# Hybrid encoder block: the first stage reordered, two gates by channels of x ahead of the memory's products

## The chip, the cores and the metric

One core of one Trainium2 chip runs the whole kernel in one launch. The metric is the device time in microseconds of one execution. TensorE (PE) does the matrix products, VectorE (DVE), ScalarE (ACT) and GpSimd (POOL) the elementwise work, and SyncE (SP) issues most of the transfers. PEld is TensorE's weight load.

## The reference

All arithmetic is float32. T = 1024 frames of D = 1024 channels, a memory of 256 tokens. Cut to what the first stage serves:

```
h = rmsnorm(x) * g                                  # x: (1024, 1024)
z = h @ w_in        # HGRN2 q, f, i, g; FoX q, k, v, f; memory q; 3 x 1024 gate logits
y_a = hgrn2(...)    # gated linear recurrence, 4 heads
y_b = fox(...)      # forgetting attention, 8 heads
mem_kv = (rmsnorm(mem) * gm) @ mem_kv_w             # 256 x 1024: keys and values
y_c = cross_attention(q, rmsnorm(keys), values)     # 4 heads
gates = sigmoid(gate_logits)                        # one per branch and channel
x = x + (sum of gate * (y @ w_branch)) @ w_out
x = x + convglu(rmsnorm(x) * gf)                    # up, causal conv of width 3, gelu, down
```

## The kernel before

**Precision.** Each float32 operand is split into a rounded high part (a cast, mostly on ScalarE) and a low part (a subtraction on VectorE). A product is three matmuls of 512 columns: high x high, high x low, low x high (`mm3`, lines 155 to 157). So each operand costs a pass on ScalarE and one on VectorE before TensorE can use it, and the second matmul needs the low part of the moving side.

**First stage.** It makes the operands `uh`, `ul` of x times its norm gain from the eight channel chunks `xk[k]` (128 channels x 1024 frames); the keys and values of the memory (`kv_chunk`: eight chunks of weights `wkv`, the first four for the keys, the others for the values; two banks of PSUM take each); the logits of the first two gates in `ORDER`, eight steps over the channel chunks (`gate_step`: two gates, two halves of 512 frames, three matmuls, so twelve per step); and the inverse norm of the rows, `rt`, from the eight row tiles `x_row` (`x_norm`: a square with a sum on ScalarE each). `rt` is transposed on TensorE, written to DRAM and read back to all partitions as `rx` (`spread_dma`). A gate's logits leave PSUM only as a product with `rx` (line 420).

**Order.** `SEQ` (line 41) names the steps in the order in which they are written: `k0` to `k7` key and value chunks, `x0` to `x7` operands of x, `g0`, `g1` weights of the two gates, `s0` to `s7` gate steps, `mn` the memory's norm, `mk` and `mv` the keys and values on their way out, `mr` the memory's rows, `xn` the norm of x. The framework's scheduler then places every instruction on its engine by a simulated time, keeping the dependences; `issue_after` adds an ordering. An engine runs its instructions in the order so made. SP issues the loads: memT and the first four weight chunks first, then the rest along `SEQ`, the rows of x last. Weight chunks and rows share six buffers (`row_tile`); split weights `wh`, `wl` have three each, raw weights two.

**After it.** Two more gates (`gates_early(NCOVER)`, the cover: 48 matmuls each) run while `differences()` makes the operands T1 to T4 of a fast block scheme out of `xk`: ScalarE first multiplies the eight chunks by the norm gain (line 582), VectorE subtracts, and each difference is split. T2 and T3 come after the first gates have left PSUM (line 588). Then seven `dense_unit`s, each of seven quarter products of twelve matmuls, use them: B11, B21, T1, T2 and so on in the first.

Of the kernel before, what the change touches and what calls it, by code (L numbers as in the profile page):

```python
# [8 lines left out]
F32 = mybir.dt.float32  # L9
# [5 lines left out]
P = 128  # L15
# [13 lines left out]
NCOVER, NPAIR = 2, 10  # L29
NFOX = [0, 3, 0, 3, 0, 3, 1]  # L30
# [10 lines left out]
SEQ = ("k0 k1 k2 k3 x0 x1 g0 x2 mr g1 k4 s0 s1 x3 s2 k5 x4 mn mk s3 k6 x5 s4 k7 mv x6 s5 x7 xn s6 s7").split()  # L41
# [65 lines left out]
def tile_block(ctx: ExitStack, tc: tile.TileContext, xT, memT, x_rows, mem_rows, vec, fbias, mats, hmask, w_cm, w_hi, w_fqk, w_fv,  # L107
# [31 lines left out]
    def col(i):  # L139
        return cv[:, i:i + 1]  # L140
# [12 lines left out]
    def mm3(ps, lh, ll, rh, rl, first, last, more=False):  # L153

        PE.matmul(ps, lh, rh, start=first, stop=False, skip_group_check=more)  # L155
        PE.matmul(ps, lh, rl, start=False, stop=False, skip_group_check=more)  # L156
        PE.matmul(ps, ll, rh, start=False, stop=last, skip_group_check=more)  # L157
# [77 lines left out]
    mt = p0.tile([P, KC, NM], F32, tag="mt", name="mt")  # L235
    def row_tile(name):
        return p0.tile([P, 2 * HB], F32, tag="wkv", name=name, bufs=6)

    wkv = [row_tile(f"wkv{q}") for q in range(4)]
    mem_row = [row_tile(f"mr{i}") for i in range(2)]  # L240
    wkv += [row_tile(f"wkv{q}") for q in range(4, 8)]
    x_row = [row_tile(f"xr{i}") for i in range(6)]
    x_row += [row_tile(f"xr{i}") for i in (6, 7)]
# [8 lines left out]
    rgw = []  # L252
    for what in SEQ:
        if what[0] == "x" and what != "xn":
            k = int(what[1])
            SP.dma_start(xk[k], xT[:, k, :])
        elif what == "mr":
            for i in range(2):
                SP.dma_start(mem_row[i], mem_rows[i])
        elif what[0] == "g":  # L260
            br, j = order[int(what[1])]
            rgw.append(raw_weights(w_cm[16 + 8 * br + j], KC * P))
        elif what in ("k4", "k5", "k6", "k7"):
            q = int(what[1])
            SP.dma_start(wkv[q], w_mkv[q])
    SP.dma_start(ident, mats[:, 0:P])
    for i in range(8):
        last_row = SP.dma_start(x_row[i], x_rows[i])
    G.memset(mhalf, -0.5)
# [34 lines left out]
    for k in range(KC):  # L304
        S.activation(umh[:, k, :], mt[:, k, :], AF.Copy, scale=col(C_GM + k))
        V.scalar_tensor_tensor(out=uml[:, k, :], in0=mt[:, k, :], scalar=col(C_GM + k),
                               in1=umh[:, k, :].bitcast(F32), op0=ALU.mult, op1=ALU.subtract)
# [7 lines left out]
    def x_chunk(k):  # L315
        late["x_cast"] = S.activation(uh[k], xk[k], AF.Copy, scale=col(C_GX + k))
        V.scalar_tensor_tensor(out=ul[k], in0=xk[k], scalar=col(C_GX + k), in1=uh[k].bitcast(F32),
                               op0=ALU.mult, op1=ALU.subtract)
# [23 lines left out]
    def kv_chunk(i):  # L342

        what, q = i // 4, i % 4
        if q == 0:
            pkv[what] = [ps_proj(), ps_proj()] if what else [ps_tr(), ps_tr()]
        wh, wl = weights(None, (2, HB), wkv[i], parts=1 if i else 2)
        for kk in range(2):
            k = 2 * q + kk
            for m in range(2):  # L350
                ms = slice(m * P, (m + 1) * P)
                mm3(pkv[what][m], umh[:, k, ms], uml[:, k, ms], wh[:, kk, :], wl[:, kk, :], k == 0, k == KC - 1)
# [7 lines left out]
    def mem_keys():  # L360
# [8 lines left out]
        for m in range(2):  # L369
            V.tensor_mul(h4(mkt[:, m, :]), h4(mkt[:, m, :]), mkr[:, 4 * m:4 * m + 4].unsqueeze(2).to_broadcast([P, 4, P]))  # L370
        for hh in range(2):
            ptr = ps_tr()
# [8 lines left out]
    gw, gps = [], []  # L381

    def gate_weights(i):
        gw.append(weights(None, (KC, P), rgw[i], [p0.tile([P, KC * P], F32R, tag=t, name=t) for t in (f"gh{i}", f"gl{i}")]))
        gps.append([ps_proj(), ps_po()] if i else [ps_lg(), ps_lg()])

    def gate_step(k):
        for i in range(2):
# [8 lines left out]

    steps = dict(k=kv_chunk, x=x_chunk, g=gate_weights, s=gate_step)
    named = dict(mn=mem_norm, mk=mem_keys, mv=mem_values, xn=x_norm)
    for what in SEQ:  # L400
        if what == "mr":
            continue
        if what in named:
            named[what]()
        else:
            steps[what[0]](int(what[1]))
    p0.release()

    home = {}
# [3 lines left out]
    mqd = tc.dram_tile([4, P, T], F32, name="mqd")  # L413

# [9 lines left out]
    early = iter([i for i in range(2, len(order)) if i < 2 + NCOVER or i >= 2 + NCOVER + NPAIR])  # L424
# [8 lines left out]

# [135 lines left out]
    row = ps1.tile([P, HB], F32, tag="fe", name="row", bufs=3)  # L569
    spread_dma(rx, rt, row[:8, :P], "rx")  # L570
    for i in range(2):
        for n in range(2):
            SP.dma_start(gd[i, n], gate(n, gps[i][n]))
    first_gates = late["gate"]

    def differences():

        b = []
        for k in range(4):
            for t in (k, k + 4):  # L580
                with tc.issue_after(late["square" if t > 3 else "x_cast"].ins):
                    S.activation(xk[t], xk[t], AF.Copy, scale=col(C_GX + t))
            b.append([xk[k + 4 * c][:, n * HB:(n + 1) * HB] for c in range(2) for n in range(2)])
# [4 lines left out]
        with tc.issue_after(first_gates.ins):  # L588
# [4 lines left out]
        with tc.issue_after(first_gates.ins):  # L593
# [14 lines left out]
    cover, families = gates_early(NCOVER), differences()  # L608
    next(cover)
# [1010 lines left out]
def _layout(inp):  # L1620
# [49 lines left out]
    o["w_cm"] = chunks(cm)  # L1670

# [52 lines left out]
```

## Time and profile before

| what | value |
|---|---|
| three runs | 1705.72, 1705.95, 1706.81 us (median 1705.95) |
| profiled execution | 1707.23 us, span 1705.5 us |
| TensorE busy | 1689.9 us (99%), 8941 matmuls |
| VectorE, ScalarE, GpSimd busy | 1142.3, 808.9, 325.7 us |
| moved by DMA | 227.17 MB |

The span runs from the first to the last recorded instruction. A row of the timeline has start, duration, engine, line, operation, output and inputs, shape, count, and in brackets the idle time before it and what ended that. Matmul durations overlap, so the pace is the distance between starts. A row of `x8: a/b/c` has the shortest, median and longest duration in nanoseconds. SPq rows are the issue of a transfer.

### The profile page before, as it was taken

What the parts mean: (1) busy time and instruction counts of PE and PEld (TensorE: products, weight loads), DVE (VectorE), ACT (ScalarE), POOL (GpSimd) and SP (SyncE); (2) the same over time, 40 slices, a digit from 0 to 9 for tenths busy, and PEclk for the clock granted to TensorE, in tenths of its full rate; (3) what the DMA queues carried; (4) which work ended last, traced back from release to release, by engine and by line L of the source; (5) the groups of instructions that cost most, each with busy time, mean ns of one, the idle gap of its engine ahead of it and who ended that gap; (6) DMA issues with size and microseconds to landing.
All of it is one profiled execution on the core that took longest, in us unless ns stands there. A gap on an engine that the chain in (4) does not pass through costs nothing.

```text
span 1705.5 us, 24256 instructions
## 1 busy us (share of the span) xinstructions
PE 1689.9 (99%) x8941; PEld 1449.0 (85%) x8941; DVE 1142.3 (67%) x2044; ACT 808.9 (47%) x1436; POOL 325.7 (19%) x419
## 2 busy tenths in 40 slices
PE   8999999999999999999999999999999999999998
PEld 6888899989898998888888888788888888888887
DVE  7656545665666655786856845987787887775654
ACT  8634456655464553776531333644443444533432
POOL 0100022443433331553310000211111111100000
PEclk9999999999999999999999999999999999999999
DMA  9533232221212111100336552566445345494772
GB/s 361 182 132 112 76 133 85 77 92 45 95 53 87 52 57 56 67 28 17 102 128 210 166 185 99 161 174 173 144 146 142 118 141 155 167 357 150 244 273 87
DMA packets 83207, 227.17 MB, mean 133 GB/s; under 512 B 9728, under 2 KB 12424, under 8 KB 83088
## 3 DMA queue, kind: packets, MB, share of 16 engines
q1 hardware_dynamic: 65040, 161.12, 26.8%
q0 software_dynamic: 18048, 64.50, 13.1%
q8 instruction: 70, 1.15, 0.3%
q14 instruction: 49, 0.40, 0.1%
HBM read 180.72 MB, written 67.93 MB: 146 GB/s over the span
## 4 chain that ended last, share of the span: by engine, by line
PE 96%; DMA 2%; DVE 1%; ACT 1%; SPq 0%; issue 0%; POOL 0%; POOLq 0%; ACTq 0%
PE pp L155 21%; PE pp L157 21%; PE pp L156 21%; PE lg L157 4%; PE lg L155 4%; PE lg L156 4%; PE tr L156 2%; PE tr L157 2%; PE tr L155 2%; PE po L877 1%; PE lg L836 1%; PE lg L835 1%; PE po L876 1%; PE po L157 1%; PE po L155 1%; PE po L156 1%
## 5 line engine op out<-in xcount | busy, mean ns | idle before, releaser
L155 PE MATMUL pp<-uh,wh 128*128 128x512 f32 x412 | 163.2, 396 | 0.3 <-ACT wh L161 0.3
L156 PE MATMUL pp<-ul,wh 128*128 128x512 f32 x412 | 162.9, 395 | 0.0
L157 PE MATMUL pp<-uh,wl 128*128 128x512 f32 x412 | 162.4, 394 | 0.0
L156 PE MATMUL pp<-wl,uh 128*128 128x256 f32 (+1 forms) x512 | 146.2, 286 | 0.0
L157 PE MATMUL pp<-wh,ul 128*128 128x256 f32 (+1 forms) x512 | 145.9, 286 | 0.0
L155 PE MATMUL pp<-wh,uh 128*128 128x256 f32 (+1 forms) x512 | 145.5, 285 | 0.0
L161 ACT CAST wh<-s 128x512 fp32r<-128x512 f32 x113 | 68.4, 620 | 155.7 <-PE pp L156 77.6
L161 ACT CAST wh<-raw 128x1024 fp32r<-128x1024 f32 (+2 forms) x76 | 67.5, 890 | 101.3 <-PE pp L156 85.7
L161 ACT CAST wh<-rw 128x512 fp32r<-128x512 f32 x87 | 53.3, 620 | 97.6 <-PE pp L156 58.1
L155 PEld LDWEIGHTS pp<-wh,uh 128*128 128x128 f32 x512 | 97.3, 190 | 1.3
L156 PEld LDWEIGHTS pp<-wl,uh 128*128 128x128 f32 x512 | 97.4, 190 | 0.9
L157 PEld LDWEIGHTS pp<-wh,ul 128*128 128x128 f32 x512 | 97.4, 190 | 0.9
L1369 POOL DMA_DIRECT2D rw<-in_w_up x44 | 24.1, 555 | 384.9 <-ACT sqs L1304 163.0
L161 ACT CAST dwh<-wr 128x1024 fp32r<-128x1024 f32 (+1 forms) x41 | 40.2, 980 | 116.0 <-PE tr L156 39.2
L169 DVE TENSOR_TENSOR wl<-raw,wh 128x1024 fp32r<-128x1024 f32 (+2 forms) x75 | 78.0, 1041 | 22.0 <-ACT wh L161 21.7
L155 PEld LDWEIGHTS pp<-uh,wh 128*128 128x128 f32 x412 | 77.5, 188 | 15.3 <-ACT wh L161 0.7
L157 PEld LDWEIGHTS pp<-uh,wl 128*128 128x128 f32 x412 | 77.5, 188 | 15.1
L156 PEld LDWEIGHTS pp<-ul,wh 128*128 128x128 f32 x412 | 77.5, 188 | 14.5
L851 ACT ACTIVATE pt<-pt,st 128x128 f32<-128x128 f32 (+3 forms) x64 | 49.7, 777 | 39.8 <-DVE st L848 32.8
L169 DVE TENSOR_TENSOR dwl<-wr,dwh 128x1024 fp32r<-128x1024 f32 (+1 forms) x41 | 46.3, 1129 | 30.3 <-ACT dwh L161 30.2
L853 POOL TENSOR_SCALAR pt<-pt,st 128x128 f32<-128x128 f32 (+3 forms) x64 | 51.0, 797 | 78.0 <-DVE st L852 57.6
L161 ACT CAST ph<-tr 128x512 fp32r<-128x512 f32 (+1 forms) x80 | 41.8, 544 | 39.8 <-PE tr L865 14.5
(501 smaller groups left out, 5121.0 us busy)
## 6 DMA issues: line engine op xcount, KB each, us to landing
rw<-in_w_up POOLq DMA_DIRECT2D x44, 512.0 KB, 4.7
sd<-in_w_dn POOLq DMA_DIRECT2D x30, 512.0 KB, 6.0
br<-yd SPq DMA_DIRECT2D x30, 512.0 KB, 5.5
raw<-in_w_cm SPq DMA_DIRECT2D x26, 512.0 KB, 3.4
gd<-gt SPq DMA_DIRECT2D x48, 256.0 KB, 2.0
gt<-gd SPq DMA_DIRECT2D x48, 256.0 KB, 2.7
yd<-fc SPq DMA_DIRECT2D x44, 256.0 KB, 2.5
wr<-sd SPq DMA_DIRECT2D x20, 512.0 KB, 4.5
```

The source lines that it names most:

```text
L155: PE.matmul(ps, lh, rh, start=first, stop=False, skip_group_check=more)
L156: PE.matmul(ps, lh, rl, start=False, stop=False, skip_group_check=more)
L157: PE.matmul(ps, ll, rh, start=False, stop=last, skip_group_check=more)
L161: return S.copy(out, in_)
L169: return (sub or V).tensor_sub(l, src, h.bitcast(F32))
L835: PE.matmul(ps[:, :w], qa[i][:, tsl], kh[i][:, s0:s0 + w], start=True, stop=False)
L836: fox_sets[p][3] = PE.matmul(ps[:, :w], qa[i][:, tsl], kl[i][:, s0:s0 + w], start=False, stop=True)
L851: S.activation(pt[:, :ns], pt[:, :ns], AF.Exp, bias=st[:, 2:3], accum_out=st[:, 3:4])
L853: G.tensor_scalar(pt[:, :ns], pt[:, :ns], st[:, 3:4], 0.0, ALU.mult, ALU.add)
L876: PE.matmul(o, vhl[:, sb, :], ph[:, src], start=(sb == 0), stop=False)
L877: PE.matmul(o, vhl[:, sb, :], pl[:, src], start=False, stop=last)
L1369: late["raw"] = G.dma_start(raw[:, 2 * i:2 * i + 2, :], src[:, 2 * i:2 * i + 2, :])
```

## The change

- `SEQ` now starts with the gates: `w0 x0 s0 w1 x1 s1 ...`. The weights of both gates lie interleaved by channel in a new input `w_first` (host layout) and come in four pieces of 1, 1, 2 and 4 channel chunks (`WFIRST`); x's first two chunks come and are split in halves.
- Memory operands (`u0` to `u7`, formerly made at the start) are made between the last steps. The key chunks `k0` to `k3` follow the last step, then the keys leave PSUM (`me`), a third gate runs (`c0`, formerly the first of the cover), the first two gates leave PSUM (`ev`), the value chunks `k4` to `k7` follow (their products after the third gate's), and `mv`, `mk`.
- The transposition of `rt` stands in the third gate, after the third channel chunk of its second half.
- Loads on SP: constants, x and gate weights, memT ahead of x6, then the memory's rows, the weight chunks and x's rows in turn. Eight buffers instead of six.
- Nine products of constants (128 x 128, float32), with no reader, stand ahead of everything on TensorE (`NDULL`); GpSimd sets their two operands.
- The eight scalings of x are on GpSimd, with no ordering.

```diff
+NDULL = 9
-SEQ = ("k0 k1 k2 k3 x0 x1 g0 x2 mr g1 k4 s0 s1 x3 s2 k5 x4 mn mk s3 k6 x5 s4 k7 mv x6 s5 x7 xn s6 s7").split()
+SEQ = ("w0 x0 s0 w1 x1 s1 w2 x2 s2 x3 s3 w4 x4 s4 x5 s5 u0 u1 x6 s6 u2 u3 x7 s7 u4 u5 mn u6 u7 k0 k1 k2 k3 me xn c0 ev k4 k5 k6 k7 mv mk").split()
+WFIRST = {0: (0, 1), 1: (1, 2), 2: (2, 4), 4: (4, 8)}
...
+    G.memset(mhalf, -0.5)
+    dull = p0.tile([P, P], F32, tag="row", name="dull")
+    G.memset(dull, 0.0)
+    for _ in range(NDULL):
+        PE.matmul(ps_tr()[:, :P], mhalf[:, 0:1].to_broadcast([P, P]), dull, start=True, stop=True)
...
     SP.dma_start(cv, vec)
-    for q in range(4):
-        w = 2 if q else 1
-        for i in range(2 // w):
-            sl, ws = slice(2 * q + i, 2 * q + i + w), slice(i * HB, (i + w) * HB)
-            SP.dma_start(mt[:, sl, :], memT[:, sl, :])
-            SP.dma_start(wkv[q][:, ws], w_mkv[q][:, ws])
+    load_x(0, 2, load_first)
+    load_first(1)
+    load_x(1, 2)
+    load_first(2)
+    load_x(2)
+    load_first(4)
+    load_x(3)
+    load_x(4)
+    load_x(5)
+    SP.dma_start(mt, memT)
+    load_x(6)
+    load_x(7)
+    for i in range(2):
+        mem_row.append(row_tile(f"mr{i}"))
+        SP.dma_start(mem_row[i], mem_rows[i])
+    load_wkv(0)
+    load_wkv(1)
     SP.dma_start(ones, mats[:, P:P + 1])
...
     SP.dma_start(ident, mats[:, 0:P])
     for i in range(8):
-        last_row = SP.dma_start(x_row[i], x_rows[i])
+        load_row(i)
+        if i in (1, 2):
+            load_wkv(len(wkv))
+        if i == 2:
+            br, j = order[2]
+            cover_raw = raw_weights(w_cm[16 + 8 * br + j], KC * P)
+    for q in (4, 5, 6, 7):
+        load_wkv(q)
...
     def gate_step(k):
-        for i in range(2):
-            for n in range(2):
+        h, l = gw[k // 4]
+        for n in range(2):
+            for i in range(2):
                 sl = slice(n * HB, (n + 1) * HB)
-                mm3(gps[i][n], gw[i][0][:, k, :], gw[i][1][:, k, :], uh[k][:, sl], ul[k][:, sl], k == 0, k == KC - 1)
+                ws = slice((k % 4) * 256 + i * P, (k % 4) * 256 + (i + 1) * P)
+                mm3(gps[i][n], h[:, ws], l[:, ws], uh[k][:, sl], ul[k][:, sl], k == 0, k == KC - 1)
...
+    def first_cover():
+        wh, wl = weights(None, (KC, P), cover_raw)
+        pss = [ps_proj(), ps_proj()]
+        for n, ps in enumerate(pss):
+            sl = slice(n * HB, (n + 1) * HB)
+            for k in range(KC):
+                late["cover"] = mm3(ps, wh[:, k, :], wl[:, k, :], uh[k][:, sl], ul[k][:, sl], k == 0, k == KC - 1)
+                if (n, k) == (1, 2):
+                    with tc.issue_after(late["cover"].ins):
+                        spread_dma(rx, rt, p0.tile([P, P], F32, tag="row", name="row")[:8, :], "rx")
+        for n, ps in enumerate(pss):
+            SP.dma_start(gd[2, n], gate(n, ps))
...
     def differences():
...
             for t in (k, k + 4):
-                with tc.issue_after(late["square" if t > 3 else "x_cast"].ins):
-                    S.activation(xk[t], xk[t], AF.Copy, scale=col(C_GX + t))
+                G.tensor_scalar(xk[t], xk[t], col(C_GX + t), 0.0, ALU.mult, ALU.add)
...
-    cover, families = gates_early(NCOVER), differences()
-    next(cover)
+    families = differences()
+    with tc.issue_after(late["wkv"].ins):
+        next(cover)
```

More of the change, by code (lines that the diff above doesn't have):

```diff
@@ L345, in kv_chunk @@
         if q == 0:
-            pkv[what] = [ps_proj(), ps_proj()] if what else [ps_tr(), ps_tr()]
-        wh, wl = weights(None, (2, HB), wkv[i], parts=1 if i else 2)
+            pkv[what] = [ps_tr(), ps_tr()]
+        wh, wl = weights(None, (2, HB), wkv[i])
         for kk in range(2):
@@ L351, in kv_chunk @@
                 ms = slice(m * P, (m + 1) * P)
-                mm3(pkv[what][m], umh[:, k, ms], uml[:, k, ms], wh[:, kk, :], wl[:, kk, :], k == 0, k == KC - 1)
+                with tc.issue_after(late["cover"].ins) if what else nullcontext():
+                    mm3(pkv[what][m], umh[:, k, ms], uml[:, k, ms], wh[:, kk, :], wl[:, kk, :], k == 0, k == KC - 1)
     def mem_values():
@@ L422, in gate @@
         return gt
-    early = iter([i for i in range(2, len(order)) if i < 2 + NCOVER or i >= 2 + NCOVER + NPAIR])
+    early = iter([i for i in range(3, len(order)) if i < 2 + NCOVER or i >= 2 + NCOVER + NPAIR])
     def gates_early(count):
@@ L568, in tile_block @@
     home["pool"] = ps1
[L569 to L574, printed above, removed]
+    first_gate = late["gate"]
     def differences():
```

112 lines of the change are left out of this document (65 added, 47 removed).

## The prediction

> **What bounds the kernel now.** I read the page first (shares and chain), then TensorE's timeline over the first 90 us, then the windows of the same stretch.
>
> ```profile
> PE 1689.9 (99%) x8941; PEld 1449.0 (85%) x8941; DVE 1142.3 (67%) x2044; ACT 808.9 (47%) x1436; POOL 325.7 (19%) x419
> ...
> PE 96%; DMA 2%; DVE 1%; ACT 1%; SPq 0%; issue 0%; POOL 0%; POOLq 0%; ACTq 0%
> ```
>
> TensorE is the bound: nothing but its idle or slow time can be won. The change removes no product of the computation, so its worth is what TensorE loses in the first 90 us, before and after.
>
> ```profile
> 5.29 1.22 PE L155 MATMUL tr<-wh,umh 128*128 128x512 f32 x2 [5.29 <-ACT wh L161]
> ...
> 6.73 0.63 PE L157 MATMUL tr<-wh,uml 128*128 128x512 f32 x1
> 7.16 0.63 PE L156 MATMUL tr<-wl,umh 128*128 128x512 f32 x1
> ...
> 9.86 0.40 PE L157 MATMUL tr<-wh,uml 128*128 128x512 f32 x1
> 10.55 0.73 PE L155 MATMUL tr<-wh,umh 128*128 128x512 f32 x2 [0.29 <-ACT wh L161]
> 11.81 0.50 PE L156 MATMUL tr<-wl,umh 128*128 128x512 f32 x1 [0.53 <-DVE wl L169]
> 12.14 0.40 PE L157 MATMUL tr<-wh,uml 128*128 128x512 f32 x1
> ...
> 24.24 0.40 PE L156 MATMUL po<-ul,gh 128*128 128x512 f32 x1
> 25.16 0.50 PE L157 MATMUL po<-uh,gl 128*128 128x512 f32 x1 [0.52 <-DVE gl L169]
> ...
> 54.30 0.39 PE L155 MATMUL pp<-uh,wh 128*128 128x512 f32 x1
> ...
> 57.70 0.39 PE L155 MATMUL pp<-uh,wh 128*128 128x512 f32 x1
> ...
> 59.06 0.27 PE L323 MATMUL tr<-ident,rt 128*8 128x128 f32 x1
> ...
> 84.15 0.39 PE L157 MATMUL pp<-uh,wl 128*128 128x512 f32 x1
> 85.21 0.50 PE L155 MATMUL pp<-T2h,wh 128*128 128x512 f32 x1 [0.68 <-ACT fe L466]
> ...
> 88.31 0.39 PE L156 MATMUL lg<-ul,wh 128*128 128x512 f32 x1
> 88.97 0.50 PE L155 MATMUL pp<-uh,wh 128*128 128x512 f32 x1 [0.28 <-ACT wh L161]
> ```
>
> A row's first number is its start. From 54.30 to 57.70 stand 16 products, so one of 512 columns costs 3.40/15 = 0.227 us. The losses against that pace: 5.29 before the first product; the first chunk's twelve take 5.29 to 10.09 (9.86 and one pace), 4.80 instead of 2.72, so 2.08, at 0.43 us each at first (6.73 to 7.16); then 0.46 until 10.55; 0.81 more than two paces until 11.81; and 0.10 for the restart (11.81 to 12.14). That is 8.74. Later: 24.24 to 25.16 loses 0.69, 84.15 to 85.21 loses 0.83, 88.31 to 88.97 loses 0.43, each with a restart of 0.10: 2.25. Together **11.0 us**. What the change can win lies inside these.
>
> **Part 1: gates by channels of x first.** The first product needed a chunk of memT and half a chunk of its weights; now it needs half of x's first chunk and an eighth of the two gates' weights. Arrivals are judged by bytes moved.
>
> ```profile
> 0.00:4.00 4.00, 0.00 (x0) 0.00 (x0) 0.64 (x6) 1.83 (x3) 0.30 (x5) 1.00 0.44 139
> 4.00:6.00 2.00, 0.71 (x2) 0.50 (x2) 1.63 (x7) 1.39 (x6) 0.00 (x0) 1.00 0.94 243
> 6.00:8.00 2.00, 2.00 (x6) 1.61 (x5) 1.27 (x5) 0.61 (x1) 0.00 (x0) 1.00 0.71 253
> 8.00:10.00 2.00, 2.00 (x7) 1.48 (x5) 0.88 (x2) 1.46 (x3) 0.00 (x0) 1.00 0.99 345
> 10.00:12.00 2.00, 1.18 (x5) 0.49 (x4) 1.47 (x2) 1.40 (x3) 0.00 (x0) 1.00 1.03 403
> 12.00:16.00 4.00, 4.00 (x18) 3.26 (x18) 3.36 (x6) 3.61 (x5) 0.00 (x0) 1.00 1.03 417
> ```
>
> ```profile
> 4.62 0.62 ACT L161 CAST wh<-wkv 128x512 fp32r<-128x512 f32 x1 [0.26 <-DMA wkv<-in_w_mkv]
> ...
> 9.45 1.05 ACT L161 CAST wh<-wkv 128x1024 fp32r<-128x1024 f32 x1 [0.33 <-DMA wkv<-in_w_mkv]
> ...
> 12.10 1.05 ACT L161 CAST wh<-wkv 128x1024 fp32r<-128x1024 f32 x1 [0.35 <-DMA wkv<-in_w_mkv]
> ...
> 82.44 1.14 ACT L161 CAST T4h<-t4s 128x512 fp32r<-128x512 f32 x2
> ```
>
> ```profile
> L316 ACT ACTIVATE uh<-xk,cv x8: 1138/1151/1158, 15.3 to 33.0; 128x1024 fp32r<-128x1024 f32 x8
> L317 DVE SCALAR_TENSOR_TENSOR ul<-xk,cv,uh x8: 1277/1280/1285, 16.5 to 36.7; 128x1024 fp32r<-128x1024 f32 x8
> ```
>
> The last column (GB/s) times the width gives, cumulatively, 0.56 MB by 4 us, 1.04 by 6, 1.55 by 8, 2.24 by 10, 3.04 by 12, then 0.417 MB per us. A cast starts later than the count says: the chunk that ends 1.64 MB (counted at 8.25) was cast at 9.45, the one that ends 2.42 MB (10.45) at 12.10, so 1.2 to 1.65 us later.
>
> *Start.* The first gate weights end at 0.46 MB, as did the half chunk cast at 4.62. In the written order their cast (a quarter of 1024 columns, about 0.45) comes first, then that of half of x0 (0.62 for 512 columns): the first product at 5.7, and the second, which needs the low part from VectorE (about 0.65), at 6.35. So the start comes no sooner than 5.29.
>
> *First steps.* A step (one channel chunk, two gates, two halves) is twelve products, 2.72 us. Steps 0 and 1 end at 6.35 + 23 x 0.227 = 11.55; x1's second half (1.38 MB, 7.35 + 1.2, then 0.6 and 0.65) is there by 9.8, wanted at 10.2. Step 2 needs x2, which ends 2.16 MB: counted at 9.8, cast at 11.0 to 11.4 by the old rate. The windows from 4 to 8 us are slow (243 and 253 GB/s, one with only 0.71 of the engines' time); at the 403 of 10 to 12 it would be 4 + 1.6/0.403 + 1.2 = 9.2. Nothing shows why they are slow, so I take the middle, 10.3, with 9.2 and 11.4 as ends. Then cast 1.15 and low part 1.28 let the second product of step 2 go at 12.75, and step 2 ends at 12.75 + 11 x 0.227 = 15.25. Its 36 products are 8.17 us of work: lost 7.1, and 0.3 for three restarts, **7.4**. By the early end nothing waits for x2: 6.35 + 35 x 0.227 = 14.3, loss 6.4 with restarts; by the late end 16.35, loss 8.5. From step 3 on x comes every 0.524/0.417 = 1.26 us against 2.72, so no wait, and the loss of 24 to 25 us goes: its weights come in parts much earlier.
>
> **Part 2: constant products ahead of the data.**
>
> ```profile
> L334 PE MATMUL tr<-ident,rt x16: 271/275/275, 1081.8 to 1083.5; 128*128 128x128 f32 x16
> ```
>
> ```profile
> 0.73 0.11 POOL L269 MEMSET mhalf<- 128x16 f32 x1 [0.29 <-POOLq L1713]
> ```
>
> ```profile
> L921 POOL MEMSET A<- 128x512 f32 x2 | 1.0, 527 | 0.0
> ```
>
> The nearest operation is line 334's: eight products leave 16 records in 1.7 us, 0.11 each, so one of the new nine takes 0.23 at full pace and 0.43 to 0.45 at the slow one: 3.9 to 4.1 us for nine. They follow two memsets (0.11 from 0.73, and at most 0.53), so run from about 1.2 to 5.2, while TensorE waits anyway. Cost: nothing as long as they end before 5.7. They should spend the slow time (2.08 us lost at about 0.2 a product is some ten products, 4.3 us) on products nobody needs.
>
> The Trainium skill ("TensorE: Matmul & The Clock Gate", "What's actually happening") says the clock opens after one busy window of 3.4 us that runs freely. By it a pause between the constant products and the data can spoil the window, the slow pace could last to about 12.4, and the time would be 1704.3; the trace shows one opening only.
>
> **Part 3: x scaled on GpSimd.** ScalarE loses eight scalings of 1.14 (34 to 38 and 52 to 56 us), where it bounds nothing: worth nothing. GpSimd gets eight of the form of line 853.
>
> ```profile
> L853 POOL TENSOR_SCALAR pt<-pt,st 128x1024 f32<-128x1024 f32 x8 | 9.0, 1128 | 19.0 <-DVE st L852 12.8 <-PE tr L867 6.2
> ```
>
> ```profile
> 225.55 2.02 POOL L165 TENSOR_SCALAR mvh<-mkv 128x1024 fp32r<-128x1024 f32 x1 [0.15 <-DMA mkv<-kvd]
> ```
>
> ```profile
> 225.43 1.23 DVE L169 TENSOR_TENSOR mkl<-mkv,mkh 128x1024 fp32r<-128x1024 f32 x1 [9.24 <-POOL mkh L165]
> ```
>
> ```profile
> L306 DVE SCALAR_TENSOR_TENSOR uml<-mt,cv,umh x8: 477/479/485, 4.2 to 14.7; 128x256 fp32r<-128x256 f32 x8
> ```
>
> That is 9.0 us, to 16 at the 2.02 of a GpSimd pass beside VectorE, on an engine with 0.00 busy from 4 to 16 us; they go in the order 0, 4, 1, 5, 2, 6, 3, 7, so seven of them wait for x4 (about 17 us). T1 is wanted at 79. Hidden, and VectorE's pass beside it kept its 1.23: cost nothing.
>
> The Trainium skill ("SBUF — State Buffer", "Who interferes with whom") says that a VectorE pass with two SBUF inputs and a GpSimd pass that reads SBUF exclude each other, whichever starts first. The row agrees for GpSimd; a rival below has the other side.
>
> **Part 4: the rest of the order.** The two waits of 84 to 89 us come from differences that pile up once rx is there, with TensorE waiting for a copy queued behind ScalarE's casts of T4 (82.44).
>
> ```profile
> 64.55 1.29 DVE L420 TENSOR_TENSOR gt<-lg,rx 128x512 f32<-128x512 f32 x2 [4.07 <-DMA rx<-rx_d]
> ```
>
> ```profile
> 52.36 1.66 POOL L174 TENSOR_TENSOR rt<-rt,mhalf 128x8 f32<-128x8 f32 x1 [1.83 <-DVE rt L173]
> ```
>
> ```profile
> L395 ACT ACTIVATE xr<-xr x8: 1048/1052/1061, 40.1 to 50.9; 128x1024 f32<-128x1024 f32 x8
> ```
>
> Now: steps 3 to 7 end at 15.25 + 13.6 = 28.9, the keys' four chunks at 39.8, and the transposition of rt stands 33 products later, at 47.3. rx follows as before, 5.5 us later (59.06 to 64.55), at 52.8. T2 is wanted after that cover (50.7), the values (61.6), 0.8 of transpositions, the second cover (73.3) and three quarter products: 81.4. The work that took 64.55 to 85 fits with 8 us to spare, so both waits (1.46) go; if not, they stay. The weights moved behind x on SP's queue: the first key chunk ends 7.93 MB, counted at 23.7, split by 27.5, wanted at 28.9. The fourth ends 11.1 MB: 35, wanted 37.1; its buffer waits for the first memory row's square, done by about 26. Cost nothing, but with only 1.5 to 2 us of cover.
>
> **Sum.** 11.0 - 7.4 = 3.6 us. The profiled execution took 1707.23 (span 1705.5), so one like it would take 1703.6; the three times have a median of 1705.95, giving **1702.3**.
>
> **Rivals.**
> - *rt comes late.* The squares of x's rows (40.1 to 50.9 before) are written behind the keys' evacuation. If ScalarE runs them there, they start at 39.8 + 2.4, take 8.4 back to back or the 11.9 seen, and rt follows 2.0 later: 52.6 or 56.1. TensorE stands at its transposition from 47.3: 5.3 or 8.8 lost, 1707.6 or **1711.1**. Past 50.9 for rt the change loses. For it: the written order. Against it: before, they were written ahead of the last steps and ran elsewhere, so the order on the engines is the scheduler's, and ScalarE has room from 29 us on.
> - *Data late*: x2 at the late end, gain 2.5: **1703.4**. For it: the measured windows.
> - *The clock opens no sooner*: the real products run slow for 4.3 us from 5.7; steps 0 and 1 end at 13.2, step 2 at 15.9 instead of 15.25: **1703.0**. The change then does not do what it says.
> - *GpSimd holds VectorE up*: in steps 4 to 7 VectorE needs 1.28 + 0.48 and waits 1.13, 2.89 against 2.72, with one more for the first: 0.8 us, **1703.1**.
> - *The differences pile up again*: 1.46 stay, **1703.8**.
>
> **Chances.** What a measurement of this kernel can tell from no change is about 0.2%, 3.4 us. My forecast (1700.8 to 1702.5) 0.50; data late 0.16, clock 0.07, GpSimd 0.05, differences 0.05, all within 0.2%: 0.33; rt late 0.17, slower. The range goes down to 1700.8 (the early end, with x0 cast ahead of the weights, 0.5 sooner) and up to 1707.6, the lower price of rt late.
>
> **What would show it.** Right: real products from about 5.7, at 0.227 from the first or second step; one wait for x2 near 12; none at 24, 84 and 88; rt's transposition with no idle time before it. Wrong: a wait over 2 us anywhere from 28 to 60 us, named by rt or by key weights; products at 0.43 after 7 us; or x2's cast after 12.

## The result and the profile after

The change makes the kernel slower: 1712.55 us (median of 7 runs, 1711.43 to 1716.77) against 1706.81 (7 runs, 1705.72 to 1708.67), a ratio of 1.0034 [1.0023, 1.0046], so 5.7 us lost where 3.6 were to be won. The profiled execution after is the longest of its seven (1716.77 us, span 1715.0); the difference to the median is explained below.

The page after, busy time and chain:

```profile
PE 1698.5 (99%) x8959; PEld 1455.9 (85%) x8959; DVE 1145.6 (67%) x2047; ACT 801.3 (47%) x1431; POOL 342.7 (20%) x428
...
PE 94%; DVE 2%; DMA 2%; issue 1%; ACT 1%; POOL 0%; SPq 0%; DVEq 0%; POOLq 0%
```

VectorE has gained a share of the chain (1% to 2%) and TensorE lost 2%. TensorE's timeline after shows where (in brackets the idle time before a row and what ended it):

```profile
5.17 0.50 PE L157 MATMUL lg<-uh,wh 128*128 128x512 f32 x1 [0.66 <-ACT wh L163]
...
14.63 0.50 PE L158 MATMUL lg<-ul,wh 128*128 128x512 f32 x1 [1.35 <-DVE ul L354]
...
18.69 0.50 PE L158 MATMUL lg<-ul,wh 128*128 128x512 f32 x1 [1.00 <-DVE ul L354]
...
28.82 0.50 PE L158 MATMUL lg<-ul,wh 128*128 128x512 f32 x1 [1.67 <-DVE ul L354]
...
55.25 0.27 PE L360 MATMUL tr<-ident,rt 128*8 128x128 f32 x1
...
85.34 0.50 PE L159 MATMUL lg<-T1h,wl 128*128 128x512 f32 x1 [1.00 <-DVE wl L171]
...
90.75 0.50 PE L158 MATMUL pp<-T2l,wh 128*128 128x512 f32 x1 [0.76 <-DVE T2l L171]
...
93.40 0.79 PE L157 MATMUL pp<-T3h,wh 128*128 128x512 f32 x1 [1.92 <-ACT wh L163]
...
95.63 0.63 PE L159 MATMUL pp<-T3h,wl 128*128 128x512 f32 x1
96.06 0.63 PE L157 MATMUL pp<-T3h,wh 128*128 128x512 f32 x1
```

Three things are new. Three waits for a low part of x, `ul`, from VectorE (4.0 us). Three waits of 85 to 94 us (3.7 us, before 0.96). And products 0.43 us apart behind the last of them (95.63 to 96.06). Counted against 0.2267 us for each product of 512 columns, TensorE has lost 9.9 us by 44.6 us before (start, idle time, restarts, slow products; the prediction's list leaves out some tenths of restarts) and 11.7 after. The low part that ended the first wait stands in VectorE's timeline after:

```profile
12.69 0.69 DVE L645 TENSOR_TENSOR xk<-xk 128x512 f32<-128x512 f32 x1 [0.95 <-POOL xk L642]
13.30 1.28 DVE L354 SCALAR_TENSOR_TENSOR ul<-xk,cv,uh 128x1024 fp32r<-128x1024 f32 x1
...
16.75 0.69 DVE L645 TENSOR_TENSOR xk<-xk 128x512 f32<-128x512 f32 x1 [1.03 <-POOL xk L642]
17.35 2.48 DVE L354 SCALAR_TENSOR_TENSOR ul<-xk,cv,uh 128x1024 fp32r<-128x1024 f32 x2
20.85 0.69 DVE L645 TENSOR_TENSOR xk<-xk 128x512 f32<-128x512 f32 x1 [1.02 <-POOL xk L642]
21.46 2.07 DVE L354 SCALAR_TENSOR_TENSOR ul<-xk,cv,uh 128x1024 fp32r<-128x1024 f32 x1
23.45 4.12 DVE L340 SCALAR_TENSOR_TENSOR uml<-mt,cv,umh 128x256 fp32r<-128x256 f32 x8
27.49 2.47 DVE L354 SCALAR_TENSOR_TENSOR ul<-xk,cv,uh 128x1024 fp32r<-128x1024 f32 x2
```

Line 645 is T1's subtraction. It reads chunks that GpSimd has scaled, so it waits for GpSimd; and the schedule puts it ahead of the next `ul`, which then waits behind it although its own input has long been there. The eight low parts of the memory (`uml`) stand ahead of another. On ScalarE and GpSimd after:

```profile
10.88 1.15 ACT L353 ACTIVATE uh<-xk,cv 128x1024 fp32r<-128x1024 f32 x1 [0.61 <-DMA xk<-in_xT]
```

```profile
10.63 2.02 POOL L642 TENSOR_SCALAR xk<-xk,cv 128x1024 f32<-128x1024 f32 x1 [1.70 <-DVE ul L354]
14.67 2.04 POOL L642 TENSOR_SCALAR xk<-xk,cv 128x1024 f32<-128x1024 f32 x1 [2.02 <-DVE ul L354]
```

The high part of x2 was done by 12.03; its low part began at 13.30. Later, VectorE again, after and then before:

```profile
61.27 1.29 DVE L460 TENSOR_TENSOR gt<-pp,rx 128x512 f32<-128x512 f32 x2 [3.74 <-DMA rx<-rx_d]
...
71.28 0.69 DVE L171 TENSOR_TENSOR wl<-raw,wh 128x512 fp32r<-128x512 f32 x1 [1.06 <-ACT wh L163]
...
74.96 0.69 DVE L540 TENSOR_TENSOR s<-raw 128x512 f32<-128x512 f32 x1 [1.46 <-DMA kvd<-mvf]
75.57 1.29 DVE L171 TENSOR_TENSOR T1l<-xk,T1h 128x512 fp32r<-128x512 f32 x2
...
90.02 0.68 DVE L171 TENSOR_TENSOR T2l<-xk,T2h 128x512 fp32r<-128x512 f32 x1
...
92.01 0.69 DVE L540 TENSOR_TENSOR s<-raw 128x512 f32<-128x512 f32 x1
```

```profile
57.99 2.49 DVE L169 TENSOR_TENSOR T1l<-xk,T1h 128x512 fp32r<-128x512 f32 x4
64.55 1.29 DVE L420 TENSOR_TENSOR gt<-lg,rx 128x512 f32<-128x512 f32 x2 [4.07 <-DMA rx<-rx_d]
...
79.32 1.28 DVE L169 TENSOR_TENSOR T2l<-xk,T2h 128x512 fp32r<-128x512 f32 x2
```

Before, T1 was split in the gap ahead of `rx`, and T2's last low part ended 16.0 us after the first gate (80.6). After, the gates stand ahead of T1: `rx` comes 3.3 us sooner, T1's split starts 17.6 us later, T2's ends 10.1 us later (90.7). The product of T3 that waits until 93.40 does not wait for T3, whose low parts end at 82.87, but for its weights. They are cast by ScalarE from a sum (`s`) that stands behind T2 on VectorE, at 92.01:

```profile
92.73 0.62 ACT L163 CAST wh<-s 128x512 fp32r<-128x512 f32 x1 [0.63 <-DVE s L540]
```

### The profile page after: what moved, and what is told of

It reads as the page before. It is cut to its first block, busy times and chain, and to the rows that moved or that the text cites. A ratio compares the mean times of both kernels' runs of the same rounds, so it can differ in the third digit from the quotient of the medians.

```text
span 1715.0 us, 24291 instructions
## 1 busy us (share of the span) xinstructions
PE 1698.5 (99%) x8959; PEld 1455.9 (85%) x8959; DVE 1145.6 (67%) x2047; ACT 801.3 (47%) x1431; POOL 342.7 (20%) x428
## 4 chain that ended last, share of the span: by engine, by line
PE 94%; DVE 2%; DMA 2%; issue 1%; ACT 1%; POOL 0%; SPq 0%; DVEq 0%; POOLq 0%
PE pp L157 20%; PE pp L158 20%; PE pp L159 20%; PE lg L158 4%; PE lg L157 4%; PE lg L159 4%; PE tr L157 3%; PE tr L158 3%; PE tr L159 3%; PE po L938 1%; PE lg L897 1%; PE lg L896 1%; PE po L937 1%; PE tr L925 1%; PE lg L1127 1%
## 5 line engine op out<-in xcount | busy, mean ns | idle before, releaser
L914 POOL TENSOR_SCALAR pt<-pt,st 128x128 f32<-128x128 f32 (+3 forms) x64 | 51.6, 806 | 78.1 <-DVE st L913 64.0
L902 DVE CUSTOM_DVE_ANT_0 pt<-lg,nf 128x512 f32<-128x512 f32 (+2 forms) x80 | 41.5, 526 | 28.4 <-PE lg L897 14.1
```

What stands on the lines that cost most here:

```text
L902: V.tensor_tensor_reduce(out=pt[:, s0 + lo:s0 + hi], in0=ps[:, lo:hi], in1=bias, op0=ALU.add, op1=ALU.max, scale=1.0, scalar=-3e38, accum_ ...
L914: G.tensor_scalar(pt[:, :ns], pt[:, :ns], st[:, 3:4], 0.0, ALU.mult, ALU.add)
```

## The experiments

All are timed beside the kernel before; "loss" is TensorE's by 44.6 us as above.

**Who holds up the low parts of x?** x scaled on ScalarE again, and T1's subtractions ordered behind the last low part of x:

```diff
 e1_act_scale
-                G.tensor_scalar(xk[t], xk[t], col(C_GX + t), 0.0, ALU.mult, ALU.add)
+                with tc.issue_after(late["square" if t > 3 else "x_cast"].ins):
+                    S.activation(xk[t], xk[t], AF.Copy, scale=col(C_GX + t))
...
 e2_t1_late
-            V.tensor_sub(b11, b11, b12)
+            with tc.issue_after(late["x_low"].ins):
+                V.tensor_sub(b11, b11, b12)
```

> Part 3 undone: x is scaled on ScalarE again, behind the squares and casts; all the rest as after. Theory Q (VectorE's queue: the subtractions of T1 stand between the low parts of x and each waits for a GpSimd scaling): the subtractions leave that place, the waits of TensorE for the low parts at 14.6 and 18.7 us (1.35 and 1.00) go, the one at 28.8 (1.67, behind the low parts of the memory) stays; excess over pace between 0 and 40 us falls by about 2.4 us. Theory G (the two engines hold each other up whenever both run): the same here, since GpSimd no longer runs; this run shows only whether Part 3 is where the 2.4 us come from. ScalarE gets 8 passes of 1.14 us back; the waits at 85 to 95 us (3.7 us) stay or grow. Time about 1710, 2 to 3 us under after.

> x stays on GpSimd, but the four subtractions of T1 are ordered behind the last low part of x on VectorE. Theory Q: the waits at 14.6 and 18.7 us go just as in the kernel that scales on ScalarE, each low part starts as its high part is there; excess over pace between 0 and 40 us falls by about 2.4 us. Theory G: GpSimd's eight scalings still run beside the low parts (11 to 35 us), the low parts still take up to 2.07 instead of 1.28 us, and more than half of the 2.4 us stay. By both the wait at 28.8 us (1.67) stays, and the waits at 85 to 95 us stay.

e1: 1710.58, ratio 1.0019 [1.0011, 1.0028]. e2: 1709.28, 1.0011 [1.0002, 1.0020]. In e1 no wait for `ul` is left, but one of 1.83 for the key's weights at 30.77 takes its place, with a slow stretch behind it (loss 11.1). In e2 the waits for `ul` shrink from 4.0 to 1.3 (0.93 of it behind the memory's low parts) and the loss to 8.9, with GpSimd still scaling. So it is the order on VectorE that costs, more than the passes on GpSimd. The groups by line of e1, then of e2, up to 42 us (busy time, mean ns):

```profile
L354 DVE SCALAR_TENSOR_TENSOR ul<-xk,cv,uh 128x1024 fp32r<-128x1024 f32 x6 | 7.5, 1283 | 1.6 <-ACT uh L353 1.5
```

```profile
L354 DVE SCALAR_TENSOR_TENSOR ul<-xk,cv,uh 128x1024 fp32r<-128x1024 f32 x6 | 9.3, 1592 | 0.6 <-ACT uh L353 0.6
```

Beside GpSimd's scalings a low part takes 1592 ns in the mean, without them 1283. That is real and smaller: 0.3 us for each of six.

**Part 3 alone**, in the kernel before (the same edit the other way):

> The kernel before with x scaled on GpSimd and nothing else (Part 3 alone, no order given to it). Cost nothing (as predicted) would be 1707.0. Theory Q: here too the subtractions of T1 stand between the low parts of x on VectorE and wait for GpSimd; the last low parts come late, TensorE waits for them between 25 and 42 us, 1 to 3 us longer in all: 1708 to 1710. Theory G: the same, but then the low parts that run beside a GpSimd pass also take longer themselves, about 2.07 instead of 1.28 us.

1710.28, 1.0024 [1.0014, 1.0033]; loss 12.1 instead of 9.9. VectorE's timeline in it:

```profile
19.81 0.69 DVE L584 TENSOR_TENSOR xk<-xk 128x512 f32<-128x512 f32 x1 [1.03 <-POOL xk L581]
20.42 2.06 DVE L169 TENSOR_TENSOR gl<-raw,gh 128x1024 fp32r<-128x1024 f32 x1
```

The same subtraction jumps in, now ahead of the gate weights' low part; TensorE waits 1.55 us for that at 22.54. The low part itself is also stretched here, 2.06 us instead of 1.22. Of the 3.7 us, 2.2 are lost by 44.6 us; most of the rest lies in the waits of 88 to 94 us (2.25 instead of 0.96). So the edit costed at nothing costs 3.7 us by itself, on a kernel without any of the other parts.

**More put behind x.** e2, with the memory's operands written behind the steps of x, their low parts also ordered behind the last of x, and several tiles elsewhere in memory:

```diff
...
+        with tc.issue_after(late["x_low"].ins):
+            V.scalar_tensor_tensor(out=uml[:, k, :], ...
...
```

> Three edits: the subtractions of T1 behind the last low part of x; the eight low parts of the memory behind them too; and the buffers of the first stage laid out so that the sums of the first family no longer lie over the buffer from which the memory's values are written out. Theory Q plus C (the differences of T are late because their casts stand in ScalarE's and VectorE's queues behind work that waits for transfers and released buffers, not because rx is late): all three waits before 40 us go (about 4 us), T1's casts come before 68 us instead of 71 and 75, and the waits of 85 to 95 us fall from 3.7 to 1.5 or less; without idle time there, the clock does not fall at 92.8 us. Time about 1705. Rival (rx at 61 us sets the differences, and layout has no part in it): the early 4 us go, the 3.7 us stay, time about 1708.

1711.11, 1.0023 [1.0014, 1.0032], worse than e2. The waits for `ul` are down to 0.2, but what was pushed back now holds up the keys:

```profile
33.71 0.79 PE L158 MATMUL tr<-wl,umh 128*128 128x512 f32 x1 [3.57 <-DVE wl L171]
```

**The constant products**: none in the changed kernel (`NDULL = 0`); the nine put into the kernel before; and there eight more between the memory's first two chunks.

> The nine constant products are left out; all else as after. If the losses simply add, the first ten or so real products run at 0.43 instead of 0.227 us and the time grows by 2.1 us, to about 1714.6. If VectorE's queue sets the pace up to 20 us (theory Q), the slow products only eat up the waits at 14.6 and 18.7 us: TensorE reaches the product that waits at 28.8 us within 0.3 us of after, and the time stays at 1712 to 1713. In the clock's rows: open at about 9.3 us instead of 4.1.

> The kernel before with nine constant products at its start and nothing else (Part 2 alone). If the slow pace is a loss of its own, its 2.08 us go: about 1705.0. If the next weights set the pace (the second weight chunk's first product waits at 10.55 us for a cast that waited for its transfer), TensorE only arrives there earlier and waits longer: the waits at 10.5 and 11.8 us grow from 1.1 to about 3 us, and the time stays at 1707.

> The kernel before with nine constant products at its start, as in the run on Part 2 alone, and eight more between the memory's first and second chunk, where TensorE waited 1.9 us for the next weights and the clock then fell to half for 3.41 us (10.77 to 14.18). Theory D (the idle time is what makes the clock fall): the clock stays open there, the products from 10.8 us on keep 0.227 us, and the time is that of before or a little under, 1706 to 1707, some 2 us under the kernel with the nine alone. Rival (the fall has another reason, such as the early opening): the clock falls again near 10.8 us, 1708.6.

e4: 1712.52, 1.0030 [1.0018, 1.0041], as the changed kernel itself. e7: 1708.65, 1.0010 [1.0001, 1.0019]. e11: 1706.87, 1.0001 [0.9992, 1.0010]. The windows of e7, then of e11 (width; TensorE's busy time first; after the engines the granted clock, DMA's share, GB/s):

```profile
7.36:10.77 3.41, 1.47 (x6) 0.78 (x6) 1.12 (x4) 2.11 (x4) 0.00 (x0) 1.00 0.98 354
10.77:14.18 3.41, 3.30 (x7) 2.13 (x8) 3.41 (x6) 3.19 (x6) 0.00 (x0) 0.50 1.04 413
```

```profile
7.36:10.77 3.41, 3.17 (x17) 2.52 (x18) 1.57 (x3) 1.48 (x4) 0.00 (x0) 1.00 1.01 387
10.77:14.18 3.41, 2.65 (x14) 2.00 (x13) 2.72 (x4) 3.31 (x6) 0.00 (x0) 1.00 1.05 418
```

In e7 the first chunk runs at full pace, and TensorE then stands until its next weights at 10.66 (1.94 us instead of 0.29). What the fast clock saves is waited away. And the granted clock falls to half in the window behind that wait. In the profiled execution of e7 (1707.07) this slow stretch costs nothing: by 44.6 us the loss is that of before. So the 2.1 us of the median stay unexplained: the four slowest of the eleven executions show a lower mean clock (0.998, the profiled one 0.999), but no trace shows where. With the gap filled (e11) the clock does not fall, and the time is that of before.

**The clock at 93 us.** Eight constant products put between T2's and T3's products in the changed kernel:

> The kernel after with eight constant products (about 1.8 us) between T2's and T3's products of the first pair, where TensorE waits 1.92 us and the clock then falls to half at 92.8 us. Theory D (idle time of about 2 us makes the clock fall): T3's wait shrinks to nearly nothing, the clock stays open there, its products take 0.23 instead of 0.43 us, and the time falls by 1.7 to 3.4 us, to 1709 to 1711; whatever happens near 239 us is not touched. Rival (the fall has another reason, or the constant products themselves delay T3): the fall stays, 1712 to 1713.

1710.71, 1.0022 [1.0012, 1.0032]. The changed kernel's windows, then e13's:

```profile
89.41:92.82 3.41, 1.32 (x5) 0.45 (x3) 3.31 (x7) 2.00 (x5) 1.04 (x2) 1.00 0.91 314
92.82:99.65 6.83, 6.25 (x14) 4.48 (x15) 6.83 (x12) 3.43 (x6) 0.00 (x0) 0.50 0.81 279
```

```profile
92.80:99.60 6.80, 6.20 (x28) 4.55 (x27) 6.80 (x12) 3.33 (x6) 0.00 (x0) 1.00 0.83 272
```

The constant products fill the wait, and T3's first product comes no sooner (93.27 against 93.40); only the fall is gone, and 1.8 us with it: half of one window of 3.41. The profiled execution after had two double windows (this one and one at 239.60), a mean clock of 0.996; the other six show 0.998 to 0.999, which leaves room for at most two single windows. At 1.7 us a window that accounts for its 4 us above the median.

**Who makes T2 and T3's weights late?** First, five kernels that bring T1 ahead: the values' products straight behind the keys' and the gates written behind T1 (e5); e5 with T1's subtractions behind `rt`'s root and the memory's load behind x (e6); the changed order with the gates written behind T1 (e9); e9 with e6's repairs (e10); e6 with x's rows loaded between the memory's weights (e12). The core of e9's edit:

```diff
+    first_gates()
+    first_gate = late["gate"]
...
-            V.tensor_add(t, a, b)
+            with tc.issue_after(late["T1l"].ins):
+                V.tensor_add(t, a, b)
```

> Only the written order of the later part of the stage is changed: the memory's values straight behind the keys (their weights loaded ahead of the rows of x), and the first gates, which wait for rx, written behind the casts of T1 as in before. Nothing is done about the first 40 us. Theory C (T1's casts are late because they are written behind gates that wait for rx and lie in memory that the values hold): T1's casts run ahead of the first gate, before 63 us instead of 71 to 76; the waits of 80 to 95 us fall from 3.7 to 1.5 or less, as in before; the clock does not fall near 92 us. The early waits (1.35, 1.00, 1.67) stay. Time about 1708. Rival (the differences are late only because rx is): rt's transposition stands about 5 us later here, rx comes at about 63 us instead of 61, so the waits of 80 to 95 us are 3.7 us or more and the time is 1712 or more.

> All three repairs: the values first and the gates behind T1 (as in the run on theory C); the subtractions of T1 behind the root for rx on VectorE, so that none stands among the low parts of x; the memory's load, casts and low parts behind those of x. Theory Q plus C: no wait over 0.6 us between 12 and 60 us, at most 1.5 us at 80 to 95 us, no fall of the clock; the excess over pace below 100 us is about 7 us against 11 in before, and the time 1703 to 1705, 2 to 4 us under before. Rival (GpSimd and VectorE hold each other up): the low parts of x still wait, 2 us or more stay before 30 us, time about 1706.

> The kernel after, with only the written order and the memory around T1 changed: the first gates and the cover's gates, which wait for rx, written behind T1's casts; the first operands and sums ordered behind T1's low parts; T1 laid over buffers that the rows of x release by 48 us. rt's transposition keeps its place among the cover's products. Theory C (the differences are late because T1's casts and low parts are queued behind work that waits for rx and for transfers): rx comes near 61 us as in after, T1's low parts by 68 us instead of 72 to 76, T2's low parts end less than 25 us behind rx instead of 29, the waits of 80 to 95 us fall from 3.7 to 1.5 or less, the clock does not fall near 92 us; the early waits stay: 1707 to 1709. Rival (rx alone sets the differences): T2's low parts still end 29 us behind rx, the 3.7 us and the fall of the clock stay, 1712.

> As the run before this one, and with the repairs of the first 40 us: T1's subtractions behind the root for rx, the memory's load, casts and low parts behind those of x. Theory Q plus C: excess over pace in the first 40 us about 5.3 us (8.7 in after), rx near 58 us, waits of 80 to 95 us at most 1.5 us, no fall of the clock before 1000 us: 1704 to 1705, about 2 us under before. Rival: as above, 1708 to 1709.

> As the run with all three repairs (values behind the keys, gates written behind T1, T1's subtractions late, the memory behind x), but with what went wrong there mended: the rows of x are loaded between the memory's weights, so that rt's transposition can stand right behind the values at about 52 us instead of 64; the keys' transpositions use a free bank instead of waiting 2.6 us for the values to be copied out; T1 lies over buffers that are free by 48 us. Theory C in its sharper form (what counts is the time from rx to the last low part of T3, 19 us in before with T1 done ahead of rx and 29 us in after): rx near 58 us, T1's low parts by 64 us, the last low parts of T2 and T3 by 80 us, no wait over 0.6 us between 60 and 100 us, no fall of the clock before 1000 us; loss in the first 40 us about 8 us as in that run: 1703 to 1705, 2 to 4 us under before. Rival (VectorE's queue finds another wait to stand at): idle time of VectorE of over 4 us between 58 and 75 us, waits of 3 us or more at 80 to 100 us, 1709 or more.

All miss, and all are slower than the change. e5: 1722.60, 1.0094 [1.0080, 1.0108]. e6: 1721.03, 1.0082 [1.0068, 1.0096]. e9: 1719.57, 1.0078 [1.0064, 1.0092]. e10: 1715.53, 1.0051 [1.0039, 1.0064]. e12: 1717.11, 1.0056 [1.0043, 1.0070]. The loss by 44.6 us is cured in e6 and e10 (8.3, 8.4); in e12 it is 7.8 ahead of a wait of 2.06 us for the values' weights that ends at 45.37. But in e9 and e10 T1's split, now at the head of VectorE's queue, waits for its own inputs with the gates behind it. In e5 and e6 it waits too (3.4 and 3.2 us), and `rt`'s transposition stands 9 to 12 us later than after (66.89 and 64.33), so these two don't test the order of VectorE alone. In e12 VectorE stands instead for weights (4.44 us) and, ahead of a sum, for a transfer (3.53). e10's VectorE:

```profile
66.33 1.30 DVE L514 TENSOR_TENSOR T1l<-xk,T1h 128x512 fp32r<-128x512 f32 x2 [5.92 <-ACT T1h L163]
71.04 0.69 DVE L459 TENSOR_TENSOR gt<-pp,rx 128x512 f32<-128x512 f32 x1 [3.41 <-PE pp L159]
```

T3's first product then waits 3.8 to 4.3 us in the five, with the clock at half behind it. Then VectorE's amount of work: four passes fewer after (T1 without its low parts; the products read its high parts in their place, so e14 leaves out T1's small term), and four more before.

```diff
 e14_less_vector
-            family_block("T1", k, b11)
+            cast(S, fam["T1"][0][:, k, :], b11)
...
 e15_before_more
+                V.tensor_sub(t4[k], b22, b12)
```

> The kernel after without T1's four low parts in the first stage (four VectorE passes of 0.6 us, 2.4 us in all); the products read T1's high parts in their place, so what is left out is the small term of T1. Theory C in its last form (VectorE's queue from rx to T3's weights is one chain, and each pass in it moves its end): the waits of 80 to 95 us fall from 3.7 to about 1.3 us, the clock does not fall near 92 us, 1707.5 to 1709.5. Rival (transfers or ScalarE set that end): the waits stay within 0.5 us of 3.7 and the time at 1712.

> The kernel before with four more VectorE passes of 128x512 (0.6 us each, their results are overwritten) among T2's differences, behind rx. Theory C in its last form: everything behind them on VectorE moves by 2.4 us, the two waits of 84 to 89 us grow from 0.96 to about 3.4 us, and with idle time of that size the clock may fall for 3.41 us (1.7 us more): 1709 to 1711. Rival (the waits of before are set by ScalarE's casts of T4 alone, VectorE has room): 1706.5 to 1707.5.

e14: 1709.37, 1.0014 [1.0005, 1.0023]. e15: 1709.57, 1.0016 [1.0007, 1.0025]. Four passes are 2.4 us (one starts 0.60 us behind another); put into the kernel before, they cost 2.8. Without them, T3's first product comes 2.2 us sooner than after (91.19 against 93.40). So VectorE sets the end of this stretch nearly one to one (15.00 of the 15 us from 80 to 95 busy in it before, 14.89 after). TensorE's wait for T3's weights in e14, then in e15:

```profile
91.19 0.50 PE L157 MATMUL pp<-T3h,wh 128*128 128x512 f32 x1 [1.28 <-ACT wh L163]
```

```profile
89.91 0.50 PE L155 MATMUL pp<-T3h,wh 128*128 128x512 f32 x1 [1.66 <-ACT wh L161]
```

Neither is followed by a fall of the clock in these two traces. That would explain why taking 2.4 us away after wins 3.2, but it is not shown: e14's profiled execution is the fastest of its eleven (1707.84, mean clock 1.000), and seven of the others show 0.999.

**The chain shortened.** T1's subtractions behind `rt`'s root, the memory's load and operands behind x, T3's subtractions ahead of `rx`, T1's casts and low parts ahead of the operands and sums of the first unit, T1 written ahead of the cover over buffers that come free early; the first two gates stay where they were:

```diff
+            with tc.issue_after(late["rstd"].ins):
+                V.tensor_sub(b11, b11, b12)
...
+        for k, (b11, b12, b21, b22) in enumerate(b):
+            with tc.issue_after(late["rstd"].ins):
+                V.tensor_sub(b12, b22, b12)
...
-        s1 = dense.sum_of(1, a21, a22)
+        with tc.issue_after(late["T1l"].ins):
+            s1 = dense.sum_of(1, a21, a22)
```

> The kernel after with the first 40 us repaired (T1's subtractions behind the root for rx, the memory's load, casts and low parts behind those of x), and with the chain from rx to the third difference's weights shortened, not only moved: T3's four subtractions, which don't need rx, done ahead of it; T1's casts and low parts ordered ahead of the operand and the sum that wait for the second half of the pair's weights and ahead of the cover's own gates; T1 and the sums laid over buffers that are free by 48 us. The first gates keep their place. Theory C: VectorE stands idle under 2 us between 58 and 90 us, T1's low parts end by 71 us, T2's by 84, the waits of 80 to 95 us are at most 0.8 us, the clock does not fall before 1000 us; the first 48 gate and key steps lose about 8 us as in the runs with that repair: 1703 to 1705, 2 to 4 us under before. Rival (one more wait at the head of VectorE's queue): waits of 2 us or more at 80 to 95 us, 1707 or more.

1704.90 (11 runs), 0.9989 [0.9980, 0.9998]: 2.0 us faster than before and 7.7 than the change, though by the bound of 0.2% hardly to be told from before. TensorE's waits up to 110 us in it (total, times, longest):

```profile
PE lg L157 <- ACT wh L163: 1.5, 2, 1.1
PE pp L159 <- DVE wl L171: 1.0, 1, 1.0
...
PE lg L158 <- DVE ul L353: 0.4, 2, 0.2
PE pp L157 <- ACT wh L163: 0.3, 1, 0.3
```

The loss is 8.0 and the clock stays up. The time came as expected, the way there did not: VectorE still idles 4.2 us between `rx` and T2 (3.4 of them for T1's cast), and about 2.4 us of waits remain at 84 to 89 us. They use up what the first 44.6 us won. The same product of T2 (the first of the second unit) starts in before, then in e16 at:

```profile
102.26 0.39 PE L155 MATMUL pp<-T2h,wh 128*128 128x512 f32 x1
```

```profile
102.30 0.39 PE L157 MATMUL pp<-T2h,wh 128*128 128x512 f32 x1
```

So by 102 us e16 has won nothing over before. Its 2.4 us in the two profiled executions come later: 0.3 by 230 us, 1.2 near 1080 us (the wait far behind, below) and 0.8 behind TensorE's last product, which starts 4.9 us before the end of the span in before and 4.0 in e16. That it beats before is luck, then: what the expectation named wins nothing over before. That it beats the change, which has the last two gains as well, comes from the repair.

## Why the prediction was wrong

**Where the 5.7 us come from.** By 44.6 us 1.8 (11.7 against 9.9). The waits of 85 to 94 us with their restarts 3.0 (4.5 against 1.5). The clock 1.8 (e13). That is 6.6. Back comes 1.2, which nothing in the prediction foresaw, from waits far behind (1.0 of idle time, the rest restarts); the windows after, then before:

```profile
1075.00:1105.00 30.00, 29.20 (x145) 24.30 (x144) 24.94 (x43) 18.45 (x35) 10.61 (x11) 1.00 0.49 145
```

```profile
1075.00:1105.00 30.00, 28.22 (x131) 23.02 (x132) 27.08 (x44) 16.97 (x30) 11.36 (x15) 1.00 0.62 184
```

Another 0.8 comes back at the end (4.0 us from the last product's start to the end of the span after, 4.9 before). The sum is 4.6 of 5.7; about 1 us is not placed, and the parts stand in single executions. Every kernel with the changed first stage idles 0.8 us in that window, every variant of before 1.8; why was not followed up.

**Part 1, half right.** The first product came at 5.17 (forecast 5.7), and x2's cast at 10.88, between the middle (10.3) and the late end (11.4); data hardly bound it (in e2 the wait there is 0.23). The step that failed is "from step 3 on x comes every 1.26 us against 2.72, so no wait": x came, its low parts did not, for VectorE was busy with work that nobody needed yet. The forecast loss was 7.4; with VectorE's order mended it is 8.0 (e16). So the gates' steps would have won nearly what was forecast, on an order that the change doesn't have.

**Part 2, wrong in what it bought.** The constant products do open the clock early (0.23 apart from 7.32 on, against 0.43 before). But "they should spend the slow time" took the 2.08 for winnable: in the kernel before the next chunk was bound by its weights at 10.5 whatever the pace (e7), and in the changed kernel without them the slow products only fill what are waits for x otherwise (e4). The opening itself came as forecast. The Trainium skill ("TensorE: Matmul & The Clock Gate", "What's actually happening") says that the clock opens after a busy window of about 3.4 us; the prediction weighed that a pause could spoil this. In the change none did; in e7 the clock opened too, and fell again at 10.77.

**Part 3, the step that failed first.** "Hidden, and VectorE's pass beside it kept its 1.23: cost nothing." It cost 3.7 us alone (e8). The rival had the place and not the mechanism: a stretched pass (2.07 at 21.46, 1.28 alone) is the small part; the large one is that a consumer of the scaled chunk, wanted at 79, was placed at 12.69 ahead of a low part wanted at 13.1 (the last product before the wait starts at 12.88), and waited there for GpSimd. The scalings did not go in the order of the sum either, seven of them behind x4 at about 17: the second began at 10.63. I asked when T1 is needed, not where its subtractions would stand. The Trainium skill ("SBUF — State Buffer", "Who interferes with whom") says that such passes exclude each other, whichever starts first; the rows show VectorE held up as well as GpSimd: 1592 ns against 1283.

**Part 4, wrong.** `rt`'s transposition ran without a wait (55.25), so the rival's price was not paid. But `rt` itself was as late as that rival said (52.6 or 56.1), at 52.97:

```profile
50.99 1.98 POOL L176 TENSOR_TENSOR rt<-rt,mhalf 128x8 f32<-128x8 f32 x1
```

`rx` was used at 61.27 instead of 52.8, because the first stage ended later (11.7 - 7.4 = 4.3), 192 products instead of 177 stand ahead of the transposition (15 x 0.227 = 3.4: all of the third gate's), and 6.0 instead of 5.5 us pass from there to the use. Whether the scheduler put the 15 ahead because of `rt` is not shown; at its forecast place the transposition would have come up at about 51.6 (47.3 + 4.3) and waited for `rt`. "The work that took 64.55 to 85 fits with 8 us to spare" counted the work behind `rx` as it was before, with T1 already done. In the changed order T1's split stands behind the gates, a sum that waits for a transfer and weights that wait for theirs: 29.4 us instead of 16.0. The rival "the differences pile up again" had the place, at a price of 1.46 (the 1.5 of before); it was 4.5, and a fall of the clock on top. The key weights came in time, as forecast.

**The clock.** That it could fall again behind a wait was in no step.

## What to carry to other kernels

Ask of every moved operation not only when its result is needed but where its consumers will stand on their engines: an instruction that is ready late, placed ahead of an urgent one on an engine that runs in order, makes the urgent one wait with it. Reordering to feed the bound engine earlier is worth something only if the next engine in the chain, here VectorE, has its urgent work first as well; count its work between the last input and the first use, in the new order. And a pause of 2 us on TensorE can cost 1.8 more behind it (e13).

## What the runs showed of the hardware

**The clock falls again in mid-run.** Stretches at half pace last a multiple of 3.41 us: mostly one such window or two (10.77 to 14.18, 92.82 to 99.65), in e10 four (89.04 to 102.69). The window of 3.41 us ahead of such a stretch need not be idle: it held 1.32 us of products in the changed kernel and 1.47 in e7. On the grid of such windows, counted from the changes of the clock, every one behind the first opening with less than 1.5 us of products was followed by half pace, in all eighteen traces; between 1.5 and 1.9 us both happened. More is not always safe: in e3 and e6 windows with 2.41 and 2.57 us of products (at 233.94 and 243.23, nearly all of 256 columns) were followed by half pace too. The Trainium skill ("TensorE: Matmul & The Clock Gate", "What's actually happening") says that the clock returns to half after an idle window of about 3.4 us; the trace agrees on the window's length and on the half, and differs on idle: a window that was 40% busy (1.32 of 3.41) is enough.

**A slow stretch that another wait swallows is free.** Without the constant products (e4) the first products run slow and the time is the same, 1712.52 against 1712.55; in e7's trace the half pace of 10.77 to 14.18 adds nothing to the loss by 44.6 us.
